# Tile starts, the order of S5, GLU and attention work, and the attention norm's steps in a fp32 encoder block on one core

## The chip, the core and the metric

The kernel runs on one core of a Trainium2 chip. The metric is the device time of one execution in microseconds (us): the median of several runs. TensorE (PE in the profile) does the matmuls and transposes, VectorE (DVE), ScalarE (ACT) and GpSimd (POOL) the work on elements, and SyncE (SP) issues most DMAs.

## The reference, cut to what matters

One layer of an encoder block on x of 1024 tokens by 1024 channels, all in float32:

```python
h = RMSNorm(x) * (1 + scale) + shift                  # scale, shift, gate = Linear(SiLU(c))
q, k, v, z_a, u, z_s, g_a, g_s = split(h @ w_in)      # 512 x6, 1024 x2 columns
# differential attention, 4 heads, v of 128 columns a head, partial rotary on q and k
p = softmax(q k^T / 8)                                # two score maps a head
o = (p[0] - lam * p[1]) @ v
o = RMSNorm(o) * (1 - lam_init)                       # per head
attn = (o * SiLU(z_a)) @ w_up_attn
# S5: 32 groups of 16 channels, 64 complex states each, scanned forward and backward over the tokens
y = gelu(s5(u, forward) + s5(u, backward) + d_skip * u)
y = y * sigmoid(y @ w_glu + b_glu)
ssm = (y * SiLU(z_s)) @ w_up_ssm
merged = sigmoid(g_a) * attn + sigmoid(g_s) * ssm
out = RMSNorm(x + gate * (merged @ w_out)) * g_final
```

## The kernel before

Every large product is float32 accuracy from three matmuls: an operand `a` is cut into `ah`, its value rounded to TensorE's short format, and `al`, the rest (`split`, line 104: a copy on ACT and a subtraction on DVE or POOL). The product is `ah bh + ah bl + al bh`. A matmul moves a tile of 128 partitions by 512 columns past 128 stationary columns. `unit` (line 209) is one block of 128 output rows: for two halves of 512 columns, `K` steps of three matmuls into a PSUM buffer `mm` of the pool `ps_mm`, then an eviction. Weights come in the fixed order of `plan` through `wr` (raw, by DMA) to `wh` and `wl`, two buffers each; `w_split` gives the subtraction to the engine in `w_state["eng"]`, V (DVE) or G (POOL).

The order of the work is written by hand. `drive(main, fill)` (line 233) runs a generator `main`, which yields amounts of time, and after each yield takes steps from `fill` until the amount is used up; a step of `unit` counts 0.66. So `yield 8.0` puts 13 steps, or 39 matmuls, of filling work there. Each engine carries out its instructions in the order in which they were written. The stages are:

- **Start:** x is loaded, normed and transposed, `hh` and `hl` are made, the first projections run.
- **S5** (`ssm_main`, line 901): eight turns, one for each set of four groups. `stage_b` makes `cb` on DVE (line 78 is the helper of all its element products) and transposes it on TensorE (line 963) for `gt`; `stage_k` multiplies `cb` (973), `stage_s` makes `sb`, `stage_d` ends in `z`, `stage_e` is the output product (lines 1048 and 1050). The fill is the projections for z and the gates.
- **GLU and the S5 up-projection** (`s2_main`, line 1194): `yh`, `yl` are cut from `ye`; `load_z` fetches a tile `zt` of SiLU(z) and multiplies it with `ye` on POOL; the GLU units are evicted by `glu_ev`, whose result is cut to `y2h`, `y2l`, which `up_ev`'s units read. `w_state["eng"]` is G from the end of S5, V from the last `split` of `yh`, and G again from the up-projection.
- **Attention** (`s3_main`, line 1520). Q, K and V of head 0 are made first; those of heads 1 to 3 are the fill (`s3_fill`), with the last gates behind them. `rope_unit` evicts a half (`rq`), rotates it (`turn`), cuts it to `rh` and the rest (`cut`), and after both halves `finish` copies them by four DMAs into `qq` or `kk`. Then 34 turns `g`, eight for each head (`h, i = divmod(g, 8)`) and two to drain. A turn holds: `qk(g)`, 8 score matmuls (1423, 1424), DVE's maxima (`nm`, 1425) and ACT's exponentials (`e`); `mix(g - 1)`, which joins the two maps on DVE; `fa` of fill; in odd turns `pv`, the product of two turns' weights with V, 24 matmuls of 256 columns (1465) into an `mm` buffer; `transpose_w(g - 1)`, 8 transposes of `e` (1454) into two buffers `tp`, cut to `wth` on ACT and `wtl` on DVE; `fb` of fill. Four spots of a turn take the work between heads by the table `EV`: `make_v` (transposes of `vt`, 1391), `o_turn` (transposes of the last head's `o`, 1478), `load_za`, `o_norm` (the norm of `o`, all of its DVE steps at one spot), `o_back` (transposes back, 1513).
- **Merge and output:** `s3_tail` ends the last head, `oh` and `ol` are multiplied with the up-projection's weights (line 217 again), `merge_ev` makes `mh`, `ml`; the output product (1707) moves `woh`, `wol` in two halves of the columns; then the last norm.

The tiles are carved out of pools one behind the other. In the built program `hh`, `hl`, `wh`, `wl`, `mh`, `ml`, `e` and the first half's `woh`, `wol` start at a multiple of 128 bytes in each partition. Past one start `woh`, `wol` of the second half (32 bytes), `oh`, `ol`, `wth`, `wtl` and `z` (64), `yh`, `yl`, `y2h`, `y2l`, `ut`, `cb` and `gt` (96).

The loop over the turns before:

```python
            spot(0, g)
            yield fa
            spot(1, g)
            if g >= 3 and g % 2 == 1:
                pv((g - 3) // 2)
            if 1 <= g <= NG:
                transpose_w(g - 1)
            spot(2, g)
            yield fb / 2
            spot(3, g)
            yield fb / 2
```

Of the kernel before, what the change touches and what calls it, by code (L numbers as in the profile page):

```python
# [18 lines left out]
P = 128  # L19
# [47 lines left out]
def tile_hybrid_block(  # L67
# [67 lines left out]
    YA, YB, YC, YL = 2.6, 4.6, 2.8, 3.0  # L135
# [229 lines left out]
    def startup():  # L365
# [16 lines left out]
        lq = pq.tile([P, 4, 64], F32, name="lq")  # L382
        dd = sp.tile([P, 8, 16], F32, name="dd")
# [336 lines left out]
        xnT = st.tile([P, KD, S], F32, name="xnT")  # L720
        junk = xq.tile([P, D], F32, name="junk")
# [179 lines left out]
    def ssm_main(t, ye):  # L901
# [65 lines left out]
        def stage_k(i):  # L967
# [9 lines left out]
            kf = hb.tile([P, 240], F32, tag="kf", bufs=1, name="kf")  # L977
# [37 lines left out]
        def stage_s(i):  # L1015
            d = st_[i]
            wv, rt = d["wv"], d["rt"]
            sb = hb.tile([P, 2, 514], F32, tag="sb", bufs=1, name="sb")
# [46 lines left out]
        yield 8.0  # L1065
# [10 lines left out]
        for i in range(NH):  # L1076
# [18 lines left out]
            yield YB  # L1095
            prev = (i,) + stage_d(i)
# [3 lines left out]
        w_state["eng"] = G  # L1100
# [93 lines left out]
    def s2_main():  # L1194
# [23 lines left out]
        sn = yp.tile([P, T * 8], F32, name="sin")  # L1218
        G.tensor_copy(out=co, in_=rt["co"])
# [15 lines left out]
        w_state["eng"] = V  # L1235
# [36 lines left out]
        w_state["eng"] = G  # L1272
# [35 lines left out]
    def rope_unit(c0, scale, h, finish):  # L1308
        t = {}

        def ev(hf, sl, ps):
# [15 lines left out]
            def cut():  # L1327
# [4 lines left out]
                sub(lo[:, sl], q, f32(hi[:, sl]), e)  # L1332

            pend.extend([turn, skip, skip, cut])
            if hf == 1:
                pend.append(lambda: finish(t["h"], lo))
        yield from unit(c0, 8, hh, hl, ev)

    def prep_q(h):
# [3 lines left out]
        def finish(hi, lo):  # L1343
            SP.dma_start(out=f32(qq[0:64, 0]), in_=f32(hi[0:64]))
            SP.dma_start(out=f32(qq[64:P, 0]), in_=f32(lo[0:64]))
            SP.dma_start(out=f32(qq[0:64, 1]), in_=f32(hi[64:P]))
            SP.dma_start(out=f32(qq[64:P, 1]), in_=f32(lo[64:P]))
            heads[h]["q_done"] = True
            if h == 0:
                turn_q(0)  # L1350
        yield from rope_unit(OQ + h * P, 0.125, h, finish)

    def prep_k(h):
# [54 lines left out]
    def qk(g):  # L1408
        h, i = divmod(g, 8)
        H = heads[h]  # L1410
        if i == 0:
            flush()
            H["zr"] = po.tile([P, 8, 2], F32, tag="zr", bufs=2, name="zr")
        tok = slice(i * P, i * P + P)
        tb = slice(i % 2 * P, i % 2 * P + P)
        nm = p3.tile([P, 2], F32, tag="nm", bufs=2, name="nm")
        zz = p3.tile([P, 2], F32, tag="zz", bufs=2, name="zz")
# [15 lines left out]
    def mix(g):  # L1433
# [3 lines left out]
        w = p3.tile([P, 1], F32, tag="wm", bufs=2, name="wm")  # L1437
# [19 lines left out]
    def pv(p):  # L1457
# [3 lines left out]
        ps = ps_mm.tile([P, 512], F32, tag="mm", name="pv")  # L1461
# [5 lines left out]
        if q == 0:  # L1467
            H["o"] = po.tile([P, S], F32, tag="o", bufs=2, name="o")
# [12 lines left out]
    def o_norm(h, e=G, big=None):  # L1481
        H = heads[h]
        on, zr = H["on"], H["zr"]
        ss = po.tile([P, 8], F32, tag="oss", name="oss")
        if big is None:
            for t in range(8):
                jk = po.tile([P, P], F32, tag="jk", name="jk")
                act(jk, on[:, t], AF.Square, scale=zr[:, t, 0:1], accum_out=ss[:, t:t + 1])
            yield
        else:  # L1490
            z2 = po.tile([P, 8], F32, tag="jk", name="z2")
            for hf in range(2):
# [295 lines left out]
```

## Time and profile before

| | before |
|---|---|
| median of 3 runs | 928.51 us (928.42 to 929.39) |
| the profiled execution | 930.2 us |
| its span | 928.3 us |
| mean granted clock of TensorE | 0.986 |
| TensorE busy | 882.2 us, 95% |
| DVE busy | 662.2 us, 71% |
| ACT busy | 375.4 us, 40% |
| POOL busy | 164.9 us, 18% |
| DMA | 119.57 MB, 129 GB/s |

The span runs from the first instruction to the last in the profile; the execution's own time has 1.9 us around it. Busy time counts an engine's instructions, overlaps once. A granted clock of 1.00 is TensorE's full clock of 2.4 GHz, 0.50 its lower one of 1.2 GHz. In the profile's rows a matmul ends when its modelled result lands, which is after the next one may have started, so distances between starts tell its pace and not the durations.

### The profile page before, as it was taken

Reading aid. Unit: us, or ns where it says so; the run is one execution under the profiler, and the core shown is the slowest. Engines: PE = TensorE matmul, PEld = TensorE weight load, DVE = VectorE, ACT = ScalarE, POOL = GpSimd, SP = SyncE. Lnnn points to the kernel's source line nnn. Section 1 sums busy time; section 2 is a strip of 40 time slices with the busy share of each in tenths; the row PEclk is TensorE's granted clock in tenths of the full one; section 3 lists DMA queues with packets and bytes.
Section 4 is the critical chain, followed back from the end, with each engine's and each line's share of the span. In section 5 each row is a group of like instructions: output and inputs, shape, how many; then the busy total and the mean of one; then the engine's idle time right before and its main releaser. Section 6 shows DMA issues by size and latency. Waiting matters only on the chain.

```text
span 928.3 us, 12225 instructions
## 1 busy us (share of the span) xinstructions
PE 882.2 (95%) x4528; PEld 731.3 (79%) x4528; DVE 662.2 (71%) x1234; ACT 375.4 (40%) x652; POOL 164.9 (18%) x128
## 2 busy tenths in 40 slices
PE   5999999999999998999999999998998999999996
PEld 4878878888888886787778877787777788888885
DVE  5987999998999964673667576755866655573465
ACT  6753532322222253301365456545645544232222
POOL 1001000000000004222234425435411111340000
PEclk9899899999999999999999999999999999999998
DMA  9926223243433554593433313313123123958022
GB/s 297 301 74 182 87 74 116 82 125 96 129 99 91 168 167 175 185 351 122 113 81 91 80 34 103 97 51 85 61 71 89 49 89 116 339 183 304 13 88 95
DMA packets 106478, 119.57 MB, mean 129 GB/s; under 512 B 7587, under 2 KB 87696, under 8 KB 106418
## 3 DMA queue, kind: packets, MB, share of 16 engines
q1 hardware_dynamic: 104628, 114.08, 40.0%
q10 hardware_dynamic: 1614, 4.51, 1.2%
q8 instruction: 36, 0.59, 0.3%
q0 software_dynamic: 176, 0.20, 0.1%
q14 instruction: 24, 0.20, 0.1%
HBM read 78.46 MB, written 27.73 MB: 114 GB/s over the span
## 4 chain that ended last, share of the span: by engine, by line
PE 68%; DVE 19%; ACT 5%; issue 3%; DMA 2%; POOL 1%; SPq 1%; ACTq 0%; DVEq 0%
PE mm L217 38%; PE op L1707 10%; PE pv L1465 5%; DVE nm L1425 3%; PE tp L1454 3%; PE sc L1423 2%; PE sc L1424 2%; ACT e L99 2%; DVE acc L96 2%; DVE cb L78 2%; PE yp L1050 1%; DVE wl L78 1%; PE w L1002 1%; DVE e L96 1%; DVE wtl L78 1%
## 5 line engine op out<-in xcount | busy, mean ns | idle before, releaser
L217 PE MATMUL mm<-hh,wh 128*128 128x512 f32 x592 | 238.1, 402 | 0.5 <-ACT o L99 0.5
L217 PE MATMUL mm<-hh,wl 128*128 128x512 f32 x592 | 232.0, 392 | 0.0
L217 PE MATMUL mm<-hl,wh 128*128 128x512 f32 x592 | 231.8, 392 | 0.0
L217 PEld LDWEIGHTS mm<-hh,wl 128*128 128x128 f32 x592 | 111.7, 189 | 24.1 <-DVE wl L78 0.5
L217 PEld LDWEIGHTS mm<-hh,wh 128*128 128x128 f32 x592 | 111.9, 189 | 23.5 <-issue 1.6
L217 PEld LDWEIGHTS mm<-hl,wh 128*128 128x128 f32 x592 | 112.0, 189 | 20.9
L99 ACT ACTIVATE e<-sc,nm 128x1024 f32<-128x1024 f32 x64 | 71.1, 1114 | 71.8 <-DVE nm L1425 71.8
L78 DVE TENSOR_TENSOR wtl<-tp,wth 128x512 fp32r<-128x512 f32 x64 | 41.2, 686 | 70.7 <-ACT wth L99 70.7
L1425 DVE TENSOR_REDUCE nm<-sc 128x1 f32<-128x1024 f32 x64 | 75.4, 1219 | 22.4 <-PE sc L1424 21.6
L78 POOL TENSOR_TENSOR wl<-wr,wh 128x1024 fp32r<-128x1024 f32 x22 | 53.5, 2430 | 185.9 <-ACT wh L99 185.8
L99 ACT ACTIVATE wh<-wr 128x1024 fp32r<-128x1024 f32 x49 | 51.7, 1057 | 64.4 <-DMA pad<-pt 21.2
L99 ACT ACTIVATE side<-mm 128x512 f32<-128x512 f32 x48 | 28.6, 597 | 107.2 <-PE mm L217 78.9
L1423 PE MATMUL sc<-kk,qq 128*128 128x512 f32 x128 | 50.6, 395 | 1.6 <-issue 1.6
L1707 PE MATMUL op<-woh,ml 128*128 128x512 f32 (+1 forms) x136 | 51.7, 380 | 0.0
L1707 PE MATMUL op<-woh,mh 128*128 128x512 f32 (+1 forms) x136 | 51.6, 380 | 0.0
L1707 PE MATMUL op<-wol,mh 128*128 128x512 f32 (+1 forms) x136 | 51.6, 380 | 0.0
L1424 PE MATMUL sc<-kk,qb 128*128 128x512 f32 x128 | 50.1, 391 | 0.0
L96 DVE SCALAR_TENSOR_TENSOR e<-e,wm 128x1024 f32<-128x1024 f32 x32 | 45.3, 1416 | 1.1
L78 DVE TENSOR_TENSOR wl<-wr,wh 128x1024 fp32r<-128x1024 f32 x27 | 32.9, 1223 | 17.9 <-ACT wh L99 17.8
L1465 PE MATMUL pv<-wth,vh 128*128 128x256 f32 x128 | 37.5, 293 | 5.5 <-ACT rq L99 2.9
L1454 PE MATMUL tp<-cst,e 128*128 128x128 f32 x256 | 33.8, 276 | 6.7 <-DVE e L96 3.9
L942 POOL MEMSET rt<- 64x4 f32 x8 | 0.8, 98 | 217.6 <-ACT rt L99 217.6
(366 smaller groups left out, 1751.7 us busy)
## 6 DMA issues: line engine op xcount, KB each, us to landing
wr<-in_w_in_dram SPq DMA_DIRECT2D x40, 512.0 KB
wa<-in_w_ada_dram SPq DMA_DIRECT2D x16, 512.0 KB
x<-in_x_dram SPq DMA_DIRECT2D x8, 512.0 KB
gsd<-side SPq DMA_DIRECT2D x8, 512.0 KB
gad<-side SPq DMA_DIRECT2D x8, 512.0 KB
gt<-gsd SPq DMA_DIRECT2D x8, 512.0 KB
wg<-in_w_ada_dram SPq DMA_DIRECT2D x8, 512.0 KB
pad<-pt ACTq DMA_DIRECT2D x8, 512.0 KB
```

Source lines behind the costliest of these rows:

```text
L78: (e or V).tensor_tensor(out=o, in0=a, in1=b, op=op)
L96: V.scalar_tensor_tensor(out=o, in0=a, scalar=s, in1=b, op0=op0, op1=op1)
L99: A.activation(out=o, in_=i, func=f, **kw)
L217: PE.matmul(out=ps, lhsT=a[:, k, off:off + P], rhs=r[:, k, sl], start=(n == 0), stop=(n == 3 * K - 1))
L1002: PE.matmul(out=wp[q][:, c4, :], lhsT=gt[:, q, c4, :], rhs=ut[:, c4, :], start=True, stop=True)
L1050: PE.matmul(out=yp[:, c4, :], lhsT=cb[:, q, c4, :, :, 1].rearrange("p t h -> p (t h)"), rhs=z[:, q, c4, :], start=False, stop=(q == 1))
L1423: PE.matmul(out=sc[:, sl], lhsT=H["qq"][:, cc, tok], rhs=H["kk"][:, cc, sl], start=True, stop=False)
L1424: PE.matmul(out=sc[:, sl], lhsT=qb_t[g // 2][:, cc, tb], rhs=H["kk"][:, cc, sl], start=False, stop=True)
L1425: V.tensor_reduce(out=nm[:, cc:cc + 1], in_=sc, axis=AX.X, op=ALU.max, negate=True)
L1454: PE.transpose(ps[:, k, :], e[:, kt * P:kt * P + P], ident)
L1465: PE.matmul(out=ps[:, 0:256], lhsT=a[:, kt, :], rhs=r[:, kt, :], start=(n == 0), stop=(n == 23))
L1707: PE.matmul(out=ps[:, 0:n], lhsT=a[:, k, tok], rhs=r[:, k, lo:lo + n], start=(i == 0), stop=(i == 23))
```

## The change

In six parts:

- **Tile starts.** Tiles named `pad`, which nothing writes or reads, are put behind small tiles in five pools, `kf` grows from 240 to 256 columns and `sb`'s rows from 514 to 528, and `nm`, `zz`, `wm` move from the pool `p3` to `po`. In the built program `woh`, `wol`, `oh`, `ol`, `yh`, `yl`, `y2h`, `y2l`, `wth`, `wtl`, `ut`, `z`, `gt`, `cb` then start at a multiple of 128 bytes.
- **S5.** The first fill is 10.5 in place of 8.0, and `stage_r`, `stage_b` of the next turn stand behind `stage_e` and its fill, not ahead of them.
- **GLU.** POOL splits no weight before attention; the product of `zt` and `ye` is made on DVE, half by half, in `glu_ev`; the loads of `zt` come behind the cuts of `yh`, those of `gt` behind the first pair of GLU units.
- **Head 0.** `finish` copies each half of Q and K as it is cut; `turn_q(0)` follows Q's first half. For the other heads `finish` copies both halves at the end, as before.
- **Attention.** In odd turns `pv` stands right behind the scores and writes a `tp` buffer. `fa` is 4.1 in even and 2.1 in odd turns up to turn 23, where it was 3.1. `make_v` and `o_turn` stand in the third turn of a head, one half of `fa` apart; `o_norm` follows in small steps, one for each spot.
- **End.** The last product of `xr` and `gf` is DVE's, not POOL's.

The diff, cut:

```diff
-    YA, YB, YC, YL = 2.6, 4.6, 2.8, 3.0
+    YF, YA, YB, YC, YL = 10.5, 2.6, 4.6, 2.8, 3.0
...
         xnT = st.tile([P, KD, S], F32, name="xnT")
+        st.tile([P, 24], F32, name="pad")
...
-        yield 8.0
+        yield YF
         stage_r(0)
         stage_b(0)
...
             stage_s(i)
             yield YA
-            if i + 1 < NH:
-                stage_r(i + 1)
-                stage_b(i + 1)
             if prev is not None:
                 stage_e(*prev)
...
             yield YB
+            if i + 1 < NH:
+                stage_r(i + 1)
+                stage_b(i + 1)
             prev = (i,) + stage_d(i)
...
-        w_state["eng"] = G
         run_all(ang)
...
                 SP.dma_start(out=zts[n], in_=zsd[n])
-                mul(zts[n], zts[n], ye[:, n] if n < 3 else t, G)
...
-        load_z(0)
-        load_z(1)
-        for m in range(3):
-            load_g(m)
         yield 2.0
         for b in range(3):
             split(yh[:, b], yl[:, b], ye[:, b])
             yield 1.5
+        load_z(0)
+        load_z(1)
         act(t[0:64], t[0:64], AF.Gelu_apprx_tanh)
...
                 sg = yq.tile([P, 512], F32, tag="sg", bufs=2, name="sg")
+                mul(zt[:, sl], zt[:, sl], (ye[:, n] if n < 3 else t)[:, sl])
                 act(sg, ps, AF.Sigmoid, bias=cols[:, CBG + n:CBG + n + 1])
...
+            if n == 0:
+                for m in range(3):
+                    load_g(m)
...
                 sub(lo[:, sl], q, f32(hi[:, sl]), e)
+                if h == 0:
+                    finish(hi, lo, sl)
...
-            if hf == 1:
-                pend.append(lambda: finish(t["h"], lo))
+            if hf == 1 and h > 0:
+                pend.append(lambda: finish(t["h"], lo, slice(0, S)))
...
-        ps = ps_mm.tile([P, 512], F32, tag="mm", name="pv")
+        ps = ps3.tile([P, 512], F32, tag="tp", bufs=2, name="pv")
...
+        for hf in range(2):
+            sl = slice(hf * 512, hf * 512 + 512)
+            if big is None:
+                jk = p3.tile([P, 512], F32, tag="tb", name="sq")
+            else:
+                jk = big[:, sl]
+            act(jk, o[:, sl], AF.Square)
+            yield
+            V.tensor_reduce(out=ss[:, 4 * hf:4 * hf + 4], in_=jk.rearrange("p (t e) -> p t e", t=4) if big is not None
+                            else jk[:].rearrange("p (t e) -> p t e", t=4), axis=AX.X, op=ALU.add)
+        mul(z2, zr[:, :, 0], zr[:, :, 0])
+        mul(ss, ss, z2)
+        yield
         res = []
-        for _ in rsqrt_gen(po, ss, 8, 1.0 / P, "o", res):
-            yield
+        for n, _ in enumerate(rsqrt_gen(po, ss, 8, 1.0 / P, "o", res)):
+            if n % 3 == 2:
+                yield
...
         make_v(0)
+        w_state["eng"] = G
...
-            if (i, s) == EV["v"] and h < 4:
+            if (i, s) == (2, 0) and h < 4:
                 make_v(h)
-            if (i, s) == EV["turn"]:
+            if (i, s) == (2, 1) and h < 4:
                 o_turn(h - 1)
...
+            odd = g % 2
+            fa += FD * (1 - 2 * odd)
             if g < NG:
                 qk(g)
             if 1 <= g <= NG:
                 mix(g - 1)
+            if g >= 3 and odd:
+                pv((g - 3) // 2)
             spot(0, g)
-            yield fa
+            yield fa / 2
             spot(1, g)
-            if g >= 3 and g % 2 == 1:
-                pv((g - 3) // 2)
+            yield fa / 2
             if 1 <= g <= NG:
                 transpose_w(g - 1)
+            yield fb / 2
             spot(2, g)
             yield fb / 2
-            spot(3, g)
-            yield fb / 2
-
-    FA, FB = 3.1, 1.0
+
+    FA, FB, FD = 3.1, 1.0, 1.0
     LA, LB = 2.45, 1.0
-    EV = {"v": (1, 3), "turn": (2, 3), "sq": (3, 3), "norm": (4, 0), "za": (5, 0), "back": (5, 3)}
...
+    fp.tile([P, 40], F32, name="pad")
...
-    mul(xg[:, 512:D], xr[t][:, 512:D], gf[:, 512:D], G)
+    mul(xg[:, 512:D], xr[t][:, 512:D], gf[:, 512:D])
```

Three places in the engines' orders. The first is TensorE's in S5, in the second turn (i = 1): the transposes of the next turn's `cb` (line 963 before, 965 after), the four pairs of `stage_e`'s product, of which one is shown, and `stage_k`'s product `kp`. Line 217 is the fill. Before:

```order
L217 MATMUL mm<-hh,wl 128x512
L963 MATMUL tp<-cst,cb 128x128 x8
L1048 MATMUL yp<-ut,m 128x128
L1050 MATMUL yp<-z,cb 128x128 x2
...
L217 MATMUL mm<-hh,wl 128x512
L973 MATMUL kp<-cb,bz 32x128 x8
```

After:

```order
L1050 MATMUL yp<-ut,m 128x128
L1052 MATMUL yp<-z,cb 128x128 x2
...
L217 MATMUL mm<-hh,wl 128x512
L965 MATMUL tp<-cst,cb 128x128 x8
L975 MATMUL kp<-cb,bz 32x128 x8
```

The transposes have moved from ahead of `stage_e` to behind it and its 21 fill matmuls; `kp` follows them at once.

The second is TensorE's in attention, in the first odd turn that has a product with V (g = 3). Before:

```order
L1423 MATMUL sc<-kk,qq 128x512
L1424 MATMUL sc<-kk,qb 128x512
L217 MATMUL mm<-hh,wh 128x512
...
L217 MATMUL mm<-hh,wl 128x512
L1465 MATMUL pv<-wth,vh 128x256
L1465 MATMUL pv<-wtl,vh 128x256
```

After:

```order
L1426 MATMUL sc<-kk,qq 128x512
L1427 MATMUL sc<-kk,qb 128x512
L1468 MATMUL pv<-wth,vh 128x256
L1468 MATMUL pv<-wtl,vh 128x256
L1468 MATMUL pv<-wth,vl 128x256
```

The fill matmuls, 15 of them, no longer stand between the scores and the product with V.

The third is ACT's in the third turn of head 2 (g = 18), from its exponentials to those of the next turn. `wh` is the hi part of a weight, `rq` and `rh` belong to a half of the next head's Q or K, `o<-tp` is `o_turn`. Before:

```order
L99 ACTIVATE e,zz<-sc,nm 128x1024 x2
L99 ACTIVATE rq<-mm 128x512
L99 ACTIVATE wh<-wr 128x1024
L99 ACTIVATE wth<-tp 128x4x128 x2
L99 ACTIVATE o<-tp 128x512 x2
L99 ACTIVATE rh<-rq 128x512
```

After:

```order
L99 ACTIVATE e,zz<-sc,nm 128x1024 x2
L99 ACTIVATE vh<-tp 128x512 x2
L99 ACTIVATE rq<-mm 128x512
L99 ACTIVATE wh<-wr 128x1024
L99 ACTIVATE o<-tp 128x512 x2
L99 ACTIVATE rh<-rq 128x512
L99 ACTIVATE wth<-tp 128x4x128 x2
L99 ACTIVATE sq<-o 128x512
```

`vh` and `o` come in ahead, and `rh` stands ahead of `wth`, which it stood behind.

## Rows read from the trace of the kernel before

**Rows 1.** The page, busy time, share of the span and instructions of each engine

```profile
PE 882.2 (95%) x4528; PEld 731.3 (79%) x4528; DVE 662.2 (71%) x1234; ACT 375.4 (40%) x652; POOL 164.9 (18%) x128
```

**Rows 2.** Time line of TensorE, output product: start, us, engine, line, operation

```profile
843.31 0.39 PE L1707 MATMUL op<-woh,mh 128*128 128x512 f32 x1
...
870.51 0.39 PE L1707 MATMUL op<-woh,mh 128*128 128x512 f32 x1
...
881.57 0.40 PE L1707 MATMUL op<-woh,mh 128*128 128x512 f32 x1
...
909.68 0.40 PE L1707 MATMUL op<-woh,mh 128*128 128x512 f32 x1
```

**Rows 3.** Time line of TensorE, first and last step of the merge

```profile
787.49 0.39 PE L217 MATMUL mm<-oh,wh 128*128 128x512 f32 x1
...
832.06 0.39 PE L217 MATMUL mm<-oh,wl 128*128 128x512 f32 x1
```

**Rows 4.** TensorE's waits, 108 to 340 us: total us, times, longest us

```profile
PE tp L963 <- DVE cb L78: 4.0, 3, 2.0
```

**Rows 5.** Windows: us, busy (instructions) of PE, PEld, DVE, ACT, POOL; clock, DMA, GB/s

```profile
178.45:203.23 24.78, 24.78 (x150) 21.06 (x146) 24.11 (x36) 7.49 (x13) 0.20 (x2) 1.00 0.42 124
356.71:360.13 3.42, 3.42 (x9) 2.63 (x8) 1.23 (x1) 2.45 (x3) 0.00 (x0) 0.50 0.52 162
```

**Rows 6.** Time line before the GLU, POOL and TensorE; in brackets idle before, releaser

```profile
347.86 5.73 POOL L78 TENSOR_TENSOR zt<-zt,ye 128x1024 f32<-128x1024 f32 x2 [5.15 <-DMA zt<-zsd]
353.56 2.33 POOL L78 TENSOR_TENSOR wl<-wr,wh 128x1024 fp32r<-128x1024 f32 x1
...
355.94 0.50 PE L217 MATMUL mm<-yh,wl 128*128 128x512 f32 x1 [2.80 <-POOL wl L78]
```

**Rows 7.** Time line at the first scores, DVE and TensorE

```profile
455.44 2.88 DVE L78 TENSOR_TENSOR rq<-rq,cosT 128x512 f32<-128x512 f32 x1
458.35 0.69 DVE L78 TENSOR_TENSOR rq<-rq,rs 128x512 f32<-128x512 f32 x1
...
466.54 0.47 PE L1423 MATMUL sc<-kk,qq 128*128 128x512 f32 x1 [1.18 <-issue]
```

**Rows 8.** TensorE's waits in attention, 465 to 770 us: total us, times, longest

```profile
PE tp L1454 <- DVE e L96: 3.9, 6, 1.2
PE pv L1465 <- ACT rq L99: 2.9, 3, 1.9
PE tp L1454 <- DVE rqv L93: 2.6, 3, 1.5
PE tp L1513 <- DVE wtl L78: 2.0, 3, 1.1
PE pv L1465 <- ACT side L99: 1.9, 2, 1.3
PE tp L1391 <- DVE wtl L78: 1.7, 3, 1.0
...
PE tp L1478 <- DVE wtl L78: 1.1, 3, 0.4
PE pv L1465 <- ACT vt L99: 0.7, 2, 0.6
```

**Rows 9.** Time line in head 2's third turn: DVE, TensorE, POOL and ACT

```profile
627.50 2.34 DVE L1425 TENSOR_REDUCE nm<-sc 128x1 f32<-128x1024 f32 x2
630.21 1.28 DVE L96 SCALAR_TENSOR_TENSOR e<-e,wm 128x1024 f32<-128x1024 f32 x1
631.64 1.06 PE L1454 MATMUL tp<-cst,e 128*128 128x128 f32 x8
632.60 2.37 POOL L78 TENSOR_TENSOR wl<-wr,wh 128x1024 fp32r<-128x1024 f32 x1 [11.13 <-ACT wh L99]
633.04 1.29 DVE L78 TENSOR_TENSOR wtl<-tp,wth 128x512 fp32r<-128x512 f32 x2 [0.59 <-ACT wth L99]
638.86 0.63 ACT L99 ACTIVATE rh<-rq 128x512 fp32r<-128x512 f32 x1 [3.13 <-POOL rq L78]
```

**Rows 10.** Time line of DVE at the end

```profile
922.59 0.78 DVE L96 SCALAR_TENSOR_TENSOR iv<-sq,cc 128x1 f32<-128x1 f32 x1 [0.58 <-ACT jk L99]
```

More of the change, by code (lines that the diff above doesn't have):

```diff
@@ L382, in startup @@
         lq = pq.tile([P, 4, 64], F32, name="lq")
+        pq.tile([P, 16], F32, name="pad")
         dd = sp.tile([P, 8, 16], F32, name="dd")
@@ L976, in stage_k @@
                               tile_position=(0, 32 * c4))
-            kf = hb.tile([P, 240], F32, tag="kf", bufs=1, name="kf")
+            kf = hb.tile([P, 256], F32, tag="kf", bufs=1, name="kf")[:, 0:240]
             act(kf[:, P:240], kp[:, 16:P], AF.Copy)
@@ L1017, in stage_s @@
             wv, rt = d["wv"], d["rt"]
-            sb = hb.tile([P, 2, 514], F32, tag="sb", bufs=1, name="sb")
+            sb = hb.tile([P, 2, 528], F32, tag="sb", bufs=1, name="sb")
             rf = rt[:].rearrange("p g j -> p (g j)")
@@ L1214, in load_z @@
                 SP.dma_start(out=zts[n], in_=zsd[n])
-                mul(zts[n], zts[n], ye[:, n] if n < 3 else t, G)
         co = yp.tile([P, T * 8], F32, name="cos")
         sn = yp.tile([P, T * 8], F32, name="sin")
+        yp.tile([P, 120], F32, name="pad")
         G.tensor_copy(out=co, in_=rt["co"])
@@ L1270, in up_ev @@
             return ev
-        w_state["eng"] = G
         for m in range(0, 8, 2):
@@ L1341, in prep_q, with finish @@
         heads.setdefault(h, {})["qq"] = qq
[L1343 to L1347, printed above, removed]
+        def finish(hi, lo, sl):
+            for cc in range(2):
+                for r, t in enumerate((hi, lo)):
+                    SP.dma_start(out=f32(qq[64 * r:64 * r + 64, cc, sl]), in_=f32(t[64 * cc:64 * cc + 64, sl]))
             heads[h]["q_done"] = True
-            if h == 0:
+            if h == 0 and sl.start == 0:
                 turn_q(0)
@@ L1412, in qk @@
             flush()
+            H["o"] = po.tile([P, S], F32, tag="o", bufs=2, name="o")
             H["zr"] = po.tile([P, 8, 2], F32, tag="zr", bufs=2, name="zr")
@@ L1415, in qk @@
         tb = slice(i % 2 * P, i % 2 * P + P)
-        nm = p3.tile([P, 2], F32, tag="nm", bufs=2, name="nm")
-        zz = p3.tile([P, 2], F32, tag="zz", bufs=2, name="zz")
+        nm = po.tile([P, 2], F32, tag="nm", bufs=2, name="nm")
+        zz = po.tile([P, 2], F32, tag="zz", bufs=2, name="zz")
         es = []
@@ L1436, in mix @@
         r = heads[h]["zr"][:, i]
-        w = p3.tile([P, 1], F32, tag="wm", bufs=2, name="wm")
+        w = po.tile([P, 1], F32, tag="wm", bufs=2, name="wm")
         V.reciprocal(out=r, in_=zz)
@@ L1466, in pv @@
                 n += 1
-        if q == 0:
-            H["o"] = po.tile([P, S], F32, tag="o", bufs=2, name="o")
         act(H["o"][:, q * 256:q * 256 + 256], ps[:, 0:256], AF.Copy)
@@ L1530, in spot @@
                 return
-            if (i, s) == EV["v"] and h < 4:
+            if (i, s) == (2, 0) and h < 4:
                 make_v(h)
-            if (i, s) == EV["turn"]:
+            if (i, s) == (2, 1) and h < 4:
                 o_turn(h - 1)
-            if (i, s) == EV["za"]:
+                gens[h] = o_norm(h - 1)
+            elif h in gens and next(gens[h], gens) is gens:
+                gens.pop(h)
+            if (i, s) == (5, 0):
                 load_za(h - 1)
-            if (i, s) == EV["sq"]:
-                gens[h] = o_norm(h - 1)
-                next(gens[h])
-            if (i, s) == EV["norm"]:
-                run_all(gens[h])
-            if (i, s) == EV["back"]:
-                of = o_back(h - 1)
-                SP.dma_start(out=ofd[h - 1], in_=of)
+            if (i, s) == (6, 0):
+                assert h not in gens
+                SP.dma_start(out=ofd[h - 1], in_=o_back(h - 1))
         for g in range(NG + 2):
             fa, fb = (FA, FB) if g < 24 else (LA, LB)
+            odd = g % 2
+            fa += FD * (1 - 2 * odd)
             if g < NG:
@@ L1591, in s3_tail @@
             SP.dma_start(out=ofl[h], in_=ofd[h])
+        next(norm)
         yield 3.0
```

22 lines of the change are left out of this document (5 added, 17 removed).

## The prediction

> **What bounds the kernel now.** I read the page first, then the time line of TensorE, then the waits by stretch, then windows where a wait needed its price. The page's engine row says that TensorE is the bound: it is busy for 882.2 of 928.3 us, VectorE (DVE) for 71% [rows 1]. So time can go in two ways only: a matmul gets shorter, or TensorE waits less.
>
> The first way shows in the output product, one loop with one shape over two halves of the columns. In the first half 120 matmuls take 870.51 - 843.31 = 27.20 us, 226.7 ns each; in the second half 120 take 909.68 - 881.57 = 28.11 us, 234.3 ns [rows 2]. What differs is the moving tile: the built program puts the first half's `woh` and `wol` at a multiple of 128 bytes in a partition, the second half's 32 bytes past one. In the merge 191 steps take 832.06 - 787.49 = 44.57 us, 233.4 ns [rows 3], and its moving tiles `oh` and `ol` lie 64 bytes past one. So an odd start costs 6.7 to 7.6 ns per 512 columns.
>
> The second way shows in the waits. In the S5 stretch TensorE waits three times, 4.0 us, for DVE's `cb` [rows 4]. Before the GLU it waits 2.80 us for a weight tile that POOL splits, and then runs 3.42 us at a granted clock of 0.50 [rows 5, 6]. At the first scores it waits 1.18 us [rows 7]. In attention eight kinds of waits make 16.8 us [rows 8]. These views count from the modelled end of the matmul ahead, 0.39 us after its start, though the next one can start after 0.23; so each wait costs 0.16 us more than its row says.
>
> **Part 1, tiles at multiples of 128 bytes.** In the changed program `woh`, `wol`, `oh`, `ol`, `yh`, `yl`, `y2h`, `y2l`, `wth`, `wtl` and the S5 tiles `ut`, `z`, `gt` all start at one. Nothing is added: the pads are never written, `kf` and `sb` are read as before. Seven output tiles of 24 matmuls by 7.6 ns are 1.3 us, the last tile's 48 half-width ones by 3.8 are 0.2. The merge's 192 by 6.7 are 1.3; the 192 on `y2h` and `y2l` are taken at the same 6.7, 1.3; the 96 on `yh` and `yl` 0.6. The 384 products with V have 256 columns: half of 6.7, 1.3. For the 320 S5 products of at most 128 columns I take 0.5, between nothing and 1. Sum 6.5 us, all on the path, as TensorE is the bound; bounds 0 and 8.
>
> The Trainium skill speaks against this part: the page "SBUF — State Buffer", section "Specifications (TRN2)", gives SBUF lines of 16 bytes and a penalty for each crossing into a new line. All the old starts are multiples of 32 bytes, so by that rule this part gives nothing and the sum is 6.5 us smaller. The two halves of rows 2 speak against it; it stays as a rival below.
>
> **Part 2, S5.** The first fill grows from 8.0 to 10.5, four steps of three matmuls, 2.7 us of TensorE work ahead of the first transposes of `cb`, whose wait is 2.0 at most plus 0.16 [rows 4]. The later transposes move behind `stage_e` and 4.6 units of fill, some 7 us later; their waits, the other 2.0 us, are about 1 each. So 4.0 + 3 x 0.16 = 4.5 us go. What they cover is late DVE work: DVE is busy for 24.11 us of a 24.78 us turn [rows 5], so it cannot catch up much. But the next thing that TensorE needs from it, `z` for the next `stage_e`, comes a full turn later. ACT's copies of `gt` move along; they are wanted only some 8 us of fill later. Bounds 2.2 (only the first wait goes) and 4.5.
>
> **Part 3, the GLU's weights.** POOL multiplies `zt` and only then splits the GLU's weight [rows 6]. Now both are DVE's. DVE is the less loaded there, and it splits a weight in 1.23 us (its one instruction in the half-clock stretch [rows 5]). So the wait of 2.80 + 0.16 goes, and with it the half clock behind it, which costs half of 3.42 us: 4.7 in all. The `zt` product joins DVE's queue ahead of the `sg` product that needs it, while ACT takes the sigmoid: hidden; without that cover it would be eight products of 0.69 us [rows 7]. Its load is issued some 7 us later, behind the splits of `yh`; first wanted at the GLU's first eviction. Bounds 3.0 (the clock falls anyway) and 5.7.
>
> **Part 4, head 0.** Q and K are handed over by halves, and Q's second copy is issued after its first half, so SP's queue is past it when K comes. On DVE a product of 0.69 us took 2.88 while POOL split a weight [rows 7]; with the split on DVE (1.23) K's second half is ready about 1 us sooner. Eight DMAs more stand in SP's queue, half as large. I count the wait of 1.18 + 0.16, 1.3 us; bounds 0 and 2.
>
> **Part 5, attention, what goes.** The product with V now takes a `tp` buffer and no longer waits for ACT to empty `mm`: 2.9 + 1.9 + 0.7, seven waits, 6.6 us with their 0.16. An even turn has 18 fill matmuls ahead of its transposes where six turns waited with 12 to 15: 0.7 us more each against 3.9 + 6 x 0.16 = 4.9, so 4.1 go. The norm's twenty DVE instructions no longer stand in one row: 2.6 + 0.5. The transposes of `vt` and of the normed `o` stand behind the scores, where their buffers have long been read: 1.7 + 2.0 + 1.0. Those of `o` behind the product with V lose their old wait, 1.1 + 0.5. Sum 20.1 us [rows 8].
>
> **What comes back.** First, the transposes of `o` follow those of `vt` with only nine fills between, at 4.7 us after the scores' start (8 score matmuls and 9 fills by 0.227, 8 transposes by 0.11, which is (1.06 - 0.16) / 8 [rows 9]). Their buffer is freed by `vl` on DVE, queued behind two reductions, 2.34, and `e`, 1.28 [rows 9], and behind ACT's two exponentials and `vh`: about 6.2. So 1.45 us, three times, 4.4. Second, the first odd turn has no product with V yet and three fills fewer: 0.7. Third, in head 2's third turn ACT's `rh` now stands ahead of `wth`. In the old order `rh` ran 6.26 us after POOL began the weight split, held by the rope's chain [rows 9]. POOL starts it some 7.6 us after the scores, so `rh` runs at 13.9, `wth` and the first `wtl` end at 15.7, and the product with V, wanted at 13.4, waits 2.3. Fourth, the norm's pieces and two reductions of half a tile stand ahead of `e` in three turns: 0.5 to 1.2 each, 2.5 in all. Fifth, head 3 keeps 15 fills in some even turns, 0.4 three times. Sum 11.1; net 20.1 - 11.1 = 9.0. Bounds: 20 with none of these, 0 if they come twice as dear.
>
> **Part 6, the end.** POOL's last product held a DVE instruction on one column for 0.78 us on the last chain [rows 10]; on DVE it takes about 0.7 itself, but beside ACT's square. I take 0.5; bounds 0 and 0.7.
>
> **The sum.** 6.5 + 4.5 + 4.7 + 1.3 + 9.0 + 0.5 = 26.5 us. The profiled execution took 930.2 us (its span of 928.3 and 1.9 around it) and would take 903.7. It lies 1.7 above the median of the runs shown, 928.5, so I forecast 902.0 for the runs.
>
> **The rivals.**
> Attention gives nothing: the new waits come to 20 us. For it speaks that DVE and ACT are in a fixed order and that I found five such places by reading; against it, that the old waits on the `mm` buffers cannot come back. 902 + 9 = 911.
> Attention runs clean: the waits that I found are shortened, since one wait gives the other engines time to catch up, and the next is smaller. 902 - 9 = 893.
> The starts of tiles do not matter, and the two halves differ for another reason (DVE's work beside them): 902 + 6.5 = 908.5. Against it: the same stationary tiles serve both halves, and the merge, other work, runs at the slower pace too [rows 3]. By the page "SBUF — State Buffer" of the Trainium skill it would come out this way.
> Slower: the product with V, now right behind the scores, comes 0.7 + 1.8 us after the transposes that feed it end, where it had 3.4 us of fill more. From the start of those transposes to the end of `wtl` rows 9 show 633.04 + 1.29 - 631.64 = 2.7 us, and it is wanted 0.9 + 0.7 + 1.8 = 3.4 after it: a margin of 0.7. If ACT is held in most turns as in the one above, each of 16 products waits 2.3 and the clock falls behind each (half of 3.42, 1.7): 15 more by 4.0 are 60, time 962. It outweighs the gain from 26.5 / 15 = 1.8 us each on. Against it: in the program's order only one even turn has ACT behind POOL's chain ahead of `wth` by more than the margin.
>
> **How the numbers follow.** The forecast, within 896 to 908, has 0.54; attention gives nothing 0.20; attention clean 0.17; starts do not matter 0.05; slower 0.04. About 0.2% is what these runs tell from no change. All cases but the last are faster by far more; so faster 0.95, within 0.2% 0.01, slower 0.04. The range 892 to 912 takes in the forecast's own band and the two attention cases; it leaves out the slow one and the far ends of the bounds together.
>
> **What would show it.** The second output half at 227 ns per matmul, and the merge too; no wait of TensorE on `cb`; no row with POOL before the GLU and a granted clock of 1.00 there; no wait of the product with V on `mm`'s evictions, but one of about 2 us in head 2's fourth turn; waits of about 1.4 us ahead of the transposes of `o`. I am wrong if the halves still differ, or if the product with V waits for `wtl` or `wth` in more than a few turns.

## The result and the profile after

The changed kernel takes 911.5 us (median of 4 runs, 910.71 to 912.36) against 928.46 us: 0.9815 of it, 95% interval 0.980 to 0.983, or 17.0 us less. Its profiled execution has a span of 909.3 us, 19.0 less than before, at a mean granted clock of 0.989. The profiled execution of the kernel before lies 1.7 us above its median and that of the changed kernel 0.3 below: that is why the spans differ by 2.0 us more than the medians. The page's engine row, to be read beside [rows 1]:

```profile
PE 873.0 (96%) x4528; PEld 732.6 (81%) x4528; DVE 673.3 (74%) x1264; ACT 366.1 (40%) x610; POOL 134.5 (15%) x115
```

TensorE does the same 4528 matmuls in 9.2 us less busy time; the other 9.8 us are idle time that went.

The program falls into stages at the first matmul of a kind on TensorE's time line (the first transposes of `cb`, the first on `yh`, on `y2h`, the first scores, the first on `oh`, the first of the output). Span of each in us, for the kernels of this study:

| | start | S5 | GLU | up, head 0 | attention | merge | output, end | span |
|---|---|---|---|---|---|---|---|---|
| before | 123.61 | 228.90 | 28.00 | 83.69 | 323.29 | 44.80 | 96.05 | 928.3 |
| changed | 126.06 | 227.42 | 21.76 | 84.41 | 310.13 | 43.52 | 96.05 | 909.3 |
| starts of tiles alone | 123.06 | 228.77 | 25.66 | 82.87 | 324.07 | 43.52 | 96.32 | 924.3 |
| changed, old S5 order | 123.92 | 229.16 | 21.76 | 84.42 | 310.20 | 43.52 | 95.52 | 908.5 |
| V's product in `mm` | 126.19 | 227.61 | 21.76 | 84.48 | 311.55 | 43.52 | 95.73 | 910.8 |
| no POOL in attention | 126.32 | 223.02 | 21.76 | 84.45 | 316.91 | 43.52 | 95.36 | 911.3 |
| o's transposes later | 126.61 | 224.66 | 21.76 | 83.17 | 310.18 | 43.52 | 94.37 | 904.3 |
| a weight to DVE | 123.21 | 227.76 | 21.76 | 83.18 | 309.66 | 43.52 | 94.33 | 903.4 |
| late cut | 123.15 | 228.89 | 21.76 | 83.19 | 321.20 | 43.52 | 94.32 | 916.0 |
| late cut, o later | 125.97 | 224.50 | 21.76 | 83.19 | 319.01 | 43.52 | 94.32 | 912.3 |
| held cuts | 122.99 | 228.30 | 21.76 | 83.21 | 307.37 | 43.52 | 94.32 | 901.5 |
| held cuts, o later | 126.11 | 222.58 | 21.76 | 83.18 | 305.69 | 43.52 | 94.33 | 897.2 |

The new first fill has four steps more, 2.7 us, ahead of the first mark, so start and S5 are read together: 352.51 before and 353.48 after. S5's part gave nothing; the gain is the GLU's 6.2 us, attention's 13.2 and the merge's 1.3. Two profiled kernels with the same code in attention (the second and the fourth row) agree there to 0.1 us; start and S5 vary by more between executions.

The faster pace shows on TensorE's time line where [rows 2, 3] stood. The merge, 191 steps, and the output's second half, 120 matmuls:

```profile
769.77 0.39 PE L217 MATMUL mm<-oh,wh 128*128 128x512 f32 x1
...
813.07 0.39 PE L217 MATMUL mm<-oh,wl 128*128 128x512 f32 x1
...
863.68 0.39 PE L1712 MATMUL op<-woh,mh 128*128 128x512 f32 x1
...
890.88 0.39 PE L1712 MATMUL op<-woh,mh 128*128 128x512 f32 x1
```

That is 43.30 / 191 and 27.20 / 120, 226.7 ns each, the pace of the first half before. TensorE's waits in attention, 465 to 770 us (total, times, longest), in the place of [rows 8]:

```profile
PE tp L1479 <- DVE vl L78: 3.2, 3, 1.1
PE pv L1468 <- DVE wtl L78: 2.7, 3, 2.0
PE tp L1457 <- DVE nry L78: 2.4, 2, 1.7
PE tp L1457 <- DVE nrt L78: 2.2, 2, 1.3
PE tp L1457 <- DVE e L96: 1.1, 1, 1.1
```

(`nry` and `nrt` are pieces of the norm: these two rows are the waits in the norm's turns.) All old kinds of waits for ACT's evictions are gone, but 11.6 us of others stand there. Ahead of attention two waits are new (108 to 465 us):

```profile
PE mm L217 <- DVE wl L78: 2.8, 1, 2.8
PE mm L217 <- DVE pt L96: 1.3, 1, 1.3
```

The first stands where no wait was, late in S5. On the time lines of ACT, DVE and TensorE:

```profile
300.02 1.06 ACT L99 ACTIVATE wh<-wr 128x1024 fp32r<-128x1024 f32 x1 [6.11 <-DMA wr<-in_w_in_dram]
```

```profile
305.54 1.21 DVE L1024 TENSOR_TENSOR_SCAN sb<-rt,wv 64x512 f32<-64x512 f32 x1
...
310.79 1.23 DVE L78 TENSOR_TENSOR wl<-wr,wh 128x1024 fp32r<-128x1024 f32 x1
```

```profile
312.07 0.50 PE L217 MATMUL mm<-hh,wl 128*128 128x512 f32 x1 [2.83 <-DVE wl L78]
```

ACT has the weight's hi part at 301.1, but DVE reaches its lo part at 310.8, behind S5's products and scans with no idle time: DVE runs some 10 us behind. It had fallen back over the turns. The second turn's `cb` and its transposes, then the last turn's:

```profile
136.63 1.23 DVE L78 TENSOR_TENSOR cb<-cb,tv 128x1024 f32<-128x1024 f32 x1
...
153.02 1.11 PE L965 MATMUL tp<-cst,cb 128*128 128x128 f32 x8
...
297.42 1.23 DVE L78 TENSOR_TENSOR cb<-cb,tv 128x1024 f32<-128x1024 f32 x1
...
302.08 1.11 PE L965 MATMUL tp<-cst,cb 128*128 128x128 f32 x8
```

DVE is done 15.2 us ahead of TensorE in the one and 3.4 us in the other. The window right behind the wait has a granted clock of 0.51 for 3.20 us (columns as in [rows 5]):

```profile
313.25:316.45 3.20, 3.20 (x9) 2.53 (x8) 3.09 (x9) 0.00 (x0) 0.00 (x0) 0.51 0.00 0
```

### The profile page after: what moved, and what is told of

Same layout as the page of the kernel before. It is cut to its first block, busy times and chain, and to the rows that moved or that the text cites. A ratio compares the mean times of both kernels' runs of the same rounds, so it can differ in the third digit from the quotient of the medians.

```text
span 909.3 us, 12201 instructions
## 1 busy us (share of the span) xinstructions
PE 873.0 (96%) x4528; PEld 732.6 (81%) x4528; DVE 673.3 (74%) x1264; ACT 366.1 (40%) x610; POOL 134.5 (15%) x115
## 4 chain that ended last, share of the span: by engine, by line
PE 41%; DVE 7%; ACT 3%; DMA 2%; issue 2%; POOL 2%; SPq 0%; ACTq 0%; DVEq 0%; POOLq 0%
PE mm L217 19%; PE op L1712 9%; PE pv L1468 4%; PE tp L1457 3%; PE sc L1427 3%; PE sc L1426 2%; DVE nm L1428 2%; POOL pta L78 1%; DVE e L96 1%; ACT e L99 1%; DVE wtl L78 1%; DMA wor<-in_w_out_dram 1%; DMA pad<-pt 1%; ACT mh L99 1%; DMA pta<-pad 1%
## 5 line engine op out<-in xcount | busy, mean ns | idle before, releaser
L78 POOL TENSOR_TENSOR wl<-wr,wh 128x1024 fp32r<-128x1024 f32 x14 | 34.7, 2477 | 207.2 <-ACT wh L99 207.0
L78 DVE TENSOR_TENSOR wl<-wr,wh 128x1024 fp32r<-128x1024 f32 x35 | 42.9, 1227 | 29.2 <-ACT wh L99 29.0
L99 ACT ACTIVATE wth<-tp 128x512 fp32r<-128x512 f32 x64 | 34.8, 596 | 40.1 <-PE tp L1457 40.1
```

Of the source, the lines that this page charges most:

```text
L78: (e or V).tensor_tensor(out=o, in0=a, in1=b, op=op)
L99: A.activation(out=o, in_=i, func=f, **kw)
```

## The experiments

**Starts of tiles alone.** The kernel before with the change's pads (four, in four pools; the text above says five) and pools for tiles.

```diff
+        pq.tile([P, 16], F32, name="pad")
+        st.tile([P, 24], F32, name="pad")
+        yp.tile([P, 120], F32, name="pad")
+    fp.tile([P, 40], F32, name="pad")
-            kf = hb.tile([P, 240], F32, tag="kf", bufs=1, name="kf")
+            kf = hb.tile([P, 256], F32, tag="kf", bufs=1, name="kf")[:, 0:240]
-            sb = hb.tile([P, 2, 514], F32, tag="sb", bufs=1, name="sb")
+            sb = hb.tile([P, 2, 528], F32, tag="sb", bufs=1, name="sb")
...
-        nm = p3.tile([P, 2], F32, tag="nm", bufs=2, name="nm")
+        nm = po.tile([P, 2], F32, tag="nm", bufs=2, name="nm")
```

> The kernel before with the tile starts of the change alone; every engine's order stays. Theory: the start sets the pace of a 512-column matmul, so merge, GLU, up-projection and the second half of the output fall from 233 to 234 ns to 227 ns, some 5 us of TensorE's work. In the changed kernel the merge's 1.3 us came back as a wait for ml, so I expect that wait of about 1.3 us here too, and a span 3 to 4 us shorter: 924.5 to 925.5 us. The products with V (256 columns) ran at 117.8 ns before and 120.0 in the change: if the start does that, they run at 120 here and cost 0.8 us of it. Rival: DVE's work beside the matmuls sets the pace; then 233 to 234 ns stay, and 928.5 us.

Measured: 926.79 against 928.67 us, 0.9976 (0.9964 to 0.9988); the profiled spans differ by 4.0 us. Some 1.7 of these 4.0 are not the pace: this execution waits 1.99 us for the GLU's weight in place of 2.80 and has no stretch of half clock behind it, where [rows 5] has one of 3.42 us. The merge falls to 43.52 us with every engine's order as before, so the start of the tile does it. The output gets no shorter, as it waits for what the merge used to hide:

```profile
834.61 0.50 PE L1711 MATMUL op<-woh,ml 128*128 128x512 f32 x1 [1.13 <-DVE ml L78]
```

And the products with V get slower. The second and the last matmul of one product of 24, before the change and with the starts alone:

```profile
509.36 0.28 PE L1465 MATMUL pv<-wtl,vh 128*128 128x256 f32 x1
...
511.95 0.28 PE L1465 MATMUL pv<-wth,vl 128*128 128x256 f32 x1
```

```profile
505.52 0.28 PE L1468 MATMUL pv<-wtl,vh 128*128 128x256 f32 x1
...
508.16 0.28 PE L1468 MATMUL pv<-wth,vl 128*128 128x256 f32 x1
```

22 distances take 2.59 us before, 117.7 ns each, and 2.64 here, 120.0. With 256 columns a start at a multiple of 128 bytes costs 2.3 ns where it saves 7 with 512. The last output tile, which has 256 columns too, shows the same: 117 ns before, 120 here.

**S5's old order in the changed kernel.**

```diff
-        yield YF
+        yield 8.0
...
+            if i + 1 < NH:
+                stage_r(i + 1)
+                stage_b(i + 1)
             if prev is not None:
                 stage_e(*prev)
...
             yield YB
-            if i + 1 < NH:
-                stage_r(i + 1)
-                stage_b(i + 1)
```

> The changed kernel with S5's old order and the old first fill; all else as changed. Theory: DVE is as loaded as TensorE in S5, so what the new order saves at cb it gives back at the next thing that DVE owes, the weight tile at 312 us. Then the three waits for cb, 4.0 us, come back, the wait for wl of 2.8 us and the half clock behind it (some 1.7 us) go, and the time is the same within 1 us: 910.5 to 912.5. Rival: the wait for wl comes from something else in the change (weights left to DVE); then it stays, and the time is about 4.5 us longer, 916.

Measured: 910.45 us (909.89 to 910.71), ratio to before 0.980 (0.978 to 0.982); the changed kernel has 0.9815 (0.980 to 0.983). Start and S5 take 353.08 us. The waits from 108 to 340 us:

```profile
PE tp L965 <- DVE cb L78: 4.3, 3, 1.9
```

DVE reaches the weight of the seventh turn as soon as ACT has its hi part:

```profile
309.91 1.23 DVE L78 TENSOR_TENSOR wl<-wr,wh 128x1024 fp32r<-128x1024 f32 x1 [0.39 <-ACT wh L99]
```

The wait for `wl` is gone and those for `cb` are back: the order of S5 moves a wait and gains nothing. While TensorE waited for `cb`, DVE caught up. The first fill and the order were put back together, so the run does not tell them apart.

**V's product in `mm` again; the merge's block 6 added on DVE.**

```diff
-        ps = ps3.tile([P, 512], F32, tag="tp", bufs=2, name="pv")
+        ps = ps_mm.tile([P, 512], F32, tag="mm", name="pv")
...
-            add(pt[:, sl], pt[:, sl], sg[:, sl], G if m < 7 else V)
+            add(pt[:, sl], pt[:, sl], sg[:, sl], G if m < 6 else V)
```

> The changed kernel with two edits far apart. First, the product with V takes an mm buffer again, at its new place right behind the scores. If the buffer is what freed it, waits of about 6 us for ACT's evictions come back in attention (stretch 310.1 us to 316); if the place alone did it, at most 1 us. Second, in the merge the addition for block 6 moves from POOL to DVE: POOL's additions of 1.3 to 1.5 us each set when ml ends, so the wait of 1.1 us for ml goes and the output stage gets 1.2 us shorter; if DVE's own queue sets it, the wait stays or grows.

Measured: one run, 912.81 us. Attention takes 311.55 us, 1.4 more. Its waits come to no more than the changed kernel's (11.2 us against 11.6); what is added is a stretch of 3.41 us at a granted clock of 0.50, from 633.94 on, which costs half of it. So the place freed the product with V, and this run shows no gain from the buffer. The wait for `ml` stays at 1.1 us, so block 6 is not the cause.

**No POOL in attention; one weight of S5 to POOL.**

```diff
-            e = V if h == 0 else G
+            e = V
...
-        w_state["eng"] = G
...
-                gens[h] = o_norm(h - 1)
+                gens[h] = o_norm(h - 1, V)
...
             stage_s(i)
+            w_state["eng"] = G if i == 6 else V
             yield YA
+            w_state["eng"] = V
```

> The changed kernel with two edits far apart. First, POOL does nothing in attention: rope, weights and norm products are DVE's. Theory: the four waits of transposes in the norm's turns (nry, nrt, 4.6 us) come from the product e, which took 2.40 us beside POOL's rope products and takes 1.28 alone; without POOL they shrink to under 1 us in sum, and the wait of the product with V at 632 us, behind POOL's chain, goes too; attention 310.1 to about 305 us. Rival: the norm's own pieces on DVE hold e; then the waits stay, and DVE's extra work (0.69 us for each rope product) makes more of them, attention 312 or more. Second, the one weight of S5's seventh turn is cut by POOL: the wait of 2.8 us at 312 us and the half clock behind it go, 4.5 us, unless the lag of DVE shows at the next thing it owes.

Measured: 914.42 us, 0.9843 (0.982 to 0.987). S5 takes 223.02 us, 4.4 less, with no wait for `wl`: the weight in DVE's queue was all of that wait. A part of DVE's lag shows elsewhere: in this and five of the six kernels below TensorE waits 0.5 to 1.4 us for `z`. (With the kernels below, start and S5 take 348.7 to 352.0 us against 353.48. In three of them a stretch of 6.83 us at half clock, from 100 to 102 us on in all other executions, is missing. TensorE came to the first transposes of `cb` 3 us sooner and waited 2.5 to 2.6 us there, so DVE sets that point too, not the first fill alone.) In attention the theory fell. The waits from 465 to 775 us:

```profile
PE pv L1470 <- DVE wtl L78: 4.5, 3, 2.5
PE tp L1459 <- DVE nrt L78: 4.1, 2, 2.3
PE tp L1481 <- DVE vl L78: 3.2, 3, 1.1
PE tp L1459 <- DVE e L96: 1.7, 2, 1.1
PE tp L1459 <- DVE nry L78: 1.0, 2, 0.7
```

They come to 14.5 us, 2.9 more, and behind two of them stand stretches of 3.41 us at a granted clock of 0.50, which cost half. Attention takes 6.8 us more. The product `e` was never longer than 1.29 us here, and the waits in the norm's turns stayed all the same: DVE's own queue is too long for POOL's work as well.

**Transposes of o later; a weight to DVE.** From here on each kernel has S5's one weight on POOL as above, the up-projection's weights on POOL and all additions of the merge on DVE:

```diff
+        w_state["eng"] = G
         for m in range(0, 8, 2):
             for q in unit_pair(m * P, y2h, y2l, [up_ev(m), up_ev(m + 1)]):
...
     def s3_main():
+        w_state["eng"] = V
...
-            add(pt[:, sl], pt[:, sl], sg[:, sl], G if m < 7 else V)
+            add(pt[:, sl], pt[:, sl], sg[:, sl], V)
```

In attention the two differ. First:

```diff
+            at = 0.75 if g % 8 == 2 else 0.5
...
-            yield fa / 2
+            yield fa * at
             spot(1, g)
-            yield fa / 2
+            yield fa * (1 - at)
```

> The changed kernel with four edits in four stages, read by the stages of the trace. S5: its seventh turn's weight is cut by POOL, as in the run without POOL in attention, where the stage fell from 227.4 to 223.0 us: 223 again. Up-projection: POOL cuts its weights, as before the change; if the weight in DVE's queue made the wait of 1.3 us for pt, that wait goes. Merge: all additions on DVE; POOL's pairs of 2.88 us in the blocks before the last two hold DVE's queue by theory, and moving the last two blocks alone changed nothing, so now the wait of 1.1 us for ml goes; if DVE's queue itself is too long it stays. Attention: in the third turn of heads 1 to 3 the transposes of o stand behind 14 of the 18 fills, not behind 9. Theory: they wait for vl alone, so their three waits of 1.06 us fall to nothing, and attention goes from 310.1 to about 307; rival: the transposes of e behind them then wait as long for the buffers that ACT empties of o, and 310 stays. Sum by theory 911.5 - 4.4 - 1.5 - 1.2 - 3 = 901.5 us.

Second:

```diff
+            w_state["eng"] = V if g == 18 else G
             spot(0, g)
```

> As the run with o's transposes later, but with those at their old place; in attention instead one weight, that of head 2's third turn, is cut by DVE and not by POOL. Theory: the wait of 2.0 us of the product with V at 632 us comes from ACT's rh, which waits behind POOL's 2.4 us split and the rope products ahead of wth; with POOL's queue free of the split, rh and wth run 2.4 us sooner, and the wait falls under 0.3 us: attention 310.1 to about 308.1. Rival: wth waits for its transposes or for ACT's other work, and the wait stays. The other three stages as in that run: 223 in S5, no wait for pt, and for ml as there.

Measured: 906.26 us, 0.9748 (0.973 to 0.976), and 906.73 us, 0.9754 (0.974 to 0.977). The common edits hold: the output stage gets 1.7 us shorter without the wait for `ml` (0.3 of it is the last DMA), so POOL's additions were its cause, and not block 6's alone. The up-projection gets 1.2 us shorter; in its stage a wait of 0.7 us for POOL's `xs` takes the place of that for `pt`. In attention neither theory paid. With the later transposes the waits for `vl` shrank to 0.4, but the product with V in head 2 waited 3.35 us, with a granted clock of 0.50 behind it until 631.12, 3.12 us; with the weight on DVE it still waited 1.57. ACT's time line, first with the later transposes, then with the weight on DVE:

```profile
626.11 0.63 ACT L99 ACTIVATE rh<-rq 128x512 fp32r<-128x512 f32 x1 [5.35 <-POOL rq L78]
626.65 1.07 ACT L99 ACTIVATE wth<-tp 128x512 fp32r<-128x512 f32 x2
```

```profile
625.86 0.63 ACT L99 ACTIVATE rh<-rq 128x512 fp32r<-128x512 f32 x1 [4.94 <-POOL rq L78]
626.39 1.07 ACT L99 ACTIVATE wth<-tp 128x512 fp32r<-128x512 f32 x2
```

ACT stands idle for some 5 us ahead of `rh`, and `wth` is behind it. POOL's three rope products hold it. Without the split in POOL's queue the first of them starts only 0.3 us sooner, since it waits for DVE's shuffle `rs`. POOL, in the two kernels:

```profile
622.20 1.29 POOL L78 TENSOR_TENSOR rs<-rs,sinT 128x512 f32<-128x512 f32 x1
```

```profile
621.93 1.29 POOL L78 TENSOR_TENSOR rs<-rs,sinT 128x512 f32<-128x512 f32 x1 [10.27 <-DVE rs L1326]
```

**Late cut.** The cut of a second half comes two steps of the queue later.

```diff
-            pend.extend([turn, skip, skip, cut])
+            pend.extend([turn, skip, skip] + [skip] * (2 if h > 0 and hf == 1 else 0) + [cut])
```

> The edits in S5, up-projection and merge as in the two runs before; in attention only the cut of each second half of Q and K (ACT's rh) is written two steps of the queue later, so that in even turns from the sixth on rh no longer stands ahead of wth in ACT's order. Those two runs showed ACT idle for 4.9 and 5.4 us ahead of rh, held by POOL's rope products with or without the weight in POOL's queue, and wth right behind. Theory: ACT's order is the cause, so the waits of the product with V for wtl (0.6, 2.2 and 0.5 us in the changed kernel) go but for the last, with the half clock where one stood; attention 310.1 to about 307.3 us, total 903.5. Rival: the rest of the chain (POOL's rope) only moves the wait to another place of ACT's queue; then attention stays within 1 us of 310.

> As the run with the late cut, and o's transposes behind 14 of 18 fills as in the run for them. There the three waits for vl fell from 1.06 to 0.4 us, but the product with V in head 2 waited 1.3 us longer, since rh held wth all the same while TensorE came sooner. Theory: with rh out of the way nothing gives the gain back, attention 2 us below the late cut alone, some 305.5 us, total 901.5 us: this is the version that should beat both kernels. Rival: TensorE then waits for e or wtl in the norm's turns by as much; attention 307 us.

Measured: 918.29 us, 0.9881 (0.987 to 0.990), and with the later transposes 914.27 us, 0.9836 (0.982 to 0.985): both slower than the changed kernel. The product with V waits 0.3 us in all, as the theory has it, but the queue carries K's copies too, and they come late. The first scores of heads 1 and 2 in the late cut:

```profile
528.28 0.77 PE L1429 MATMUL sc<-kk,qq 128*128 128x512 f32 x1 [6.20 <-DMA kk<-rq]
...
608.79 0.77 PE L1429 MATMUL sc<-kk,qq 128*128 128x512 f32 x1 [4.90 <-DMA kk<-rq]
```

Behind each wait the granted clock is 0.50, from 528.28 to 532.92 and from 608.79 to 614.83 us: half of these 10.7 us comes on top.

**Held cuts.** A cut due in an even turn ahead of the transposes of `e` waits for them and is written right behind; nothing else of the queue falls back.

```diff
+    held = {"on": False, "n": 0}
+
     def pop():
-        if pend:
+        if held["on"] and pend and pend[0].__name__ == "cut":
+            held["n"] += 1
+        elif pend:
             pend.popleft()()
...
+            held["on"] = g % 2 == 0
             spot(0, g)
...
                 transpose_w(g - 1)
+            let_go()
```

(`let_go` ends the hold and makes up the pops that were held.)

> The edits in S5, up-projection and merge as before; in attention a cut that comes up in an even turn ahead of the transposes of e is held and written right behind them, so rh follows wth in every even turn and nothing else of the queue moves, the copies of K included. The late cut took the product with V's waits away but moved K's copies some four steps back, and the first scores of heads 1 and 2 waited 6.4 and 5.1 us for K. Theory: the waits for wtl stay away and K is in time: attention 310.1 to about 307.5 us, total 903.5 to 904. Rival: the late rh makes K's copy late by as much, and waits of several us for K stay ahead of a head's first scores.

> As the run with held cuts, and the transposes of o behind 14 of 18 fills. Theory: the three waits for vl fall from 1.06 to 0.4 us and nothing behind takes it back, since wth no longer waits for rh: attention 2 us below the held cuts alone, about 305.5, total 901.5 to 902. Rival: the transposes of e or the norm's turns take it back, and the two runs are equal.

Measured: 903.69 us, 0.9730 (0.971 to 0.975), attention 307.37; with the later transposes 901.67 us, 0.9715 (0.970 to 0.973), attention 305.69. Both are as expected, and the last beats both kernels. The intervals of the two overlap; that the later transposes gain is read from the attention stage, 1.7 us shorter in one profile of each. The last one's waits in attention:

```profile
PE tp L1470 <- DVE nrt L78: 2.6, 2, 1.5
PE tp L1470 <- DVE nry L78: 2.5, 2, 1.7
PE tp L1470 <- DVE e L96: 1.1, 1, 1.1
PE tp L1492 <- DVE vl L78: 0.8, 2, 0.4
PE pv L1481 <- DVE wtl L78: 0.7, 2, 0.4
```

The 2.0 us for `wtl` is gone, and two thirds of what is left is the norm's turns.

## Why the prediction was right, and where it was not

The forecast was 902.0 us within 892 to 912, and the time is 911.5: faster, inside the range, but with 17.0 of the 26.5 us. It lies at the price of the rival in which attention gives nothing, and that is not what happened: attention gave more than forecast. The forecast's own band, 896 to 908, was missed. That 911.5 lies within the range, by 0.5 us, is owed to the room left for that rival, and so to luck. The signs named ahead came: the halves at one pace, no wait on `cb`, no half clock before the GLU, one wait of 2.0 us for `wtl`, three of 1.06 us (1.4 named) ahead of the transposes of `o`.

1. **Starts (6.5).** The 512-column terms held: merge 1.28 (1.3 forecast), output 27.20 us for 120 matmuls as forecast. By the line rule of the page "SBUF — State Buffer" (section "Specifications (TRN2)") of the Trainium skill there would have been nothing; the run with the starts alone shows otherwise. Two steps failed, and one small term. "Half of 6.7" for 256 columns has the wrong sign: 384 products by 2.3 ns are 0.9 us lost, not 1.3 gained, and the 0.2 of the last output tile turned the same way. The 0.5 for S5's products did not come: `yp` runs at 111 to 113 ns before and after. And "all on the path" missed that the chain of POOL's additions and DVE's work to the last `ml` didn't get faster: the 1.3 us of the merge came back as a wait. The run shows 1.9 us by its medians; of the 4.0 by its spans 1.7 are the GLU's half clock.
2. **S5 (4.5).** This is the step that failed most: "the next thing that TensorE needs from it, `z` for the next `stage_e`, comes a full turn later". DVE also cuts the fill's weights, in the same queue. DVE's lag grew until a weight was late: 2.83 us, and half of 3.20 us at half clock. The old order is as fast; with that one weight on POOL the stage is 4.4 us shorter.
3. **GLU (4.7).** The wait for POOL's weight (3.0), its half clock (1.7), a wait of 0.83 us for ACT's `sg` at the stage's end, which I hadn't counted, and the faster pace (0.6) together are the stage's 6.2 us: it is 96 matmuls at 226.7 ns, with no wait. This is read from the traces; no run takes this part back alone. What I left out is that the up-projection's weights went to DVE too, ahead of `pt`: 1.3 us came back, and went with those weights on POOL.
4. **Head 0 (1.3).** No wait ahead of the scores is left, as forecast.
5. **Attention (9.0).** The stage is 13.2 us shorter, some 1.3 of it the head's first scores, which wait inside it. Four of the five returns came: `vl` 3.2 us in three waits (4.4 forecast), the first odd turn 1.1 (0.7), `rh` ahead of `wth` 2.0 (2.3), the norm's turns 4.6 (2.5); head 3's even turns show none. The place of the product with V, not its buffer, did the work, as far as one run can show. Before the change a wait of the product with V in head 2 had a stretch of half clock behind it, and I hadn't counted its 1.7 us; it is gone. Together the rows account for some 10 of the 13.2 us: waits 8.0 with their 0.16, the first scores 1.3, the half clock 1.7, less 0.9 for V's products. What makes the other 3 was not taken apart by a run and stays open. The stretch, a window of the kernel before:

```profile
643.43:646.85 3.42, 3.42 (x19) 3.42 (x18) 0.00 (x0) 0.06 (x1) 3.34 (x3) 0.50 0.96 229
```

6. **End (0.5).** From the last `tmp` on DVE to the issue of the last DMA it was 3.74 us, in the run with the starts alone 3.73, and is 3.37 to 3.38 in all kernels with this part: 0.4 us, nearly the term. In the changed kernel's profile the last DMA then took 0.3 us longer than in the others (3.70 against 3.40), which hides it.

The rival that was slower needed ACT to be held ahead of `wth` in most turns; it was in one, as the order said (the other two waits for `wtl` are 0.45 and 0.28 us), and ACT's idle row ahead of `rh` shows the mechanism.

## What to carry to other kernels

Where an engine off the bound is nearly as busy as the bound, as DVE in S5 (24.11 of 24.78 us), a wait for it that an order takes away can come out at the next thing in its queue: list all that it owes, not only what the edit moves, and give some of it to another engine, as the one weight to POOL. Shift work by the order of one instruction in one queue, as the held cuts do; the same cut delayed by two steps of a shared queue cost over 11 us of waits for K. Put the start of a tile that is moved in 512 columns at a multiple of 128 bytes.

## What the runs showed of the hardware

- A matmul of 512 columns takes 226.7 ns from start to start when its moving tile starts at a multiple of 128 bytes in a partition and 233 to 234 ns at 32, 64 or 96 past one; one of 256 columns 120.0 and 117.7 ns (64 past one). The run with the starts alone shows both. Why the sign turns stays open.
- A DVE product is held by a POOL product beside it: the joined map `e` took 2.40 us beside a rope product in the changed kernel, and 1.28 without one [rows 9]; in the run with no POOL work in attention all 32 took 1.28 to 1.29. A step of the norm on 8 columns, `nrt`, took 2.25 us beside POOL's split of a weight, and 0.17 in that run.

```profile
566.27 2.40 DVE L96 SCALAR_TENSOR_TENSOR e<-e,wm 128x1024 f32<-128x1024 f32 x1
566.30 1.29 POOL L78 TENSOR_TENSOR rq<-rq,rs 128x512 f32<-128x512 f32 x1
...
568.58 2.43 POOL L78 TENSOR_TENSOR wl<-wr,wh 128x1024 fp32r<-128x1024 f32 x1 [0.99 <-ACT wh L99]
568.78 2.25 DVE L96 SCALAR_TENSOR_TENSOR nrt<-nrt,rqv 128x8 f32<-128x8 f32 x1
```
